# Ten blocks of the mixer input projection split at the latent and prompt boundary: 512 and 128 columns in place of 320 and 320

## The chip, the cores and the metric

The kernel runs on one core of one Trainium2 chip. The metric is device time in microseconds (us) of one execution of the whole program. A core has a matrix engine (PE here; its weight loads are listed apart, as PEld), a vector engine (DVE), a scalar engine (ACT), GpSimd (POOL) and a sync engine (SP) that issues the transfers. Each engine works through its own instructions in order, and they wait for one another by semaphores.

## The reference, cut to what matters

Two layers work on 640 tokens with 1024 features: 512 latent tokens and 128 prompt tokens, which share all weights.

```
def trunk_layer(x, cond, p, pos, ctx_kv):
    ...
    x = x + 0.5 * g1 * swiglu(h, p['wg'][0], p['wu'][0], p['wd'][0])

    h = rmsnorm(x, p['norm'][1]) * (1 + sc2) + sh2
    u = h @ p['w_in']
    ...
    u_pool, q, k, v, u_hy = jnp.split(u, [s1, s2, s3, s4], axis=-1)
    ...
    mix = jnp.concatenate([y_pool, a, y_hy], axis=-1) @ p['w_out']
    x = x + g2 * mix
    ...
    x = x + 0.5 * g3 * swiglu(h, p['wg'][1], p['wu'][1], p['wd'][1])
```

The change is in `u = h @ p['w_in']`, which has 1792 output features: 14 blocks of 128.

## The kernel before

Activations are kept with features on the 128 partitions and the 640 tokens along the free dimension, so a product's moving operand is a slice of tokens. Products are made from float32r operands (a float32 rounded to fewer bits). For accuracy every operand is split in a rounded part and its rest, and one product is three matmuls: weight-high with input-high, weight-high with input-low, weight-low with input-high. Each matmul loads its 128x128 weights anew, also where the one before used the same.

`mul` writes one half of the tokens of one block of 128 features: for each of the 8 slices `k` of the inner dimension, three matmuls that add up in one PSUM bank. A half is `HT` = 320 tokens. `gemm_steps` takes the inner dimension in two groups of four slices. For each group it loads and splits the weights (`load_weight`: a transfer, a rounding on ACT into `whi`, a subtraction on DVE into `wlo`), then calls `mul` for the first half, 12 matmuls, and for the second, 12 more; it yields after each call, so that other work can be put between.

In `mixer`, the first `MIXSKEW` = 4 of the 14 blocks are made ahead from weights that were loaded earlier (`gemm_kept`). The other ten are made in the generator `work`: two PSUM tiles, the four calls of `mul`, and two copies on ACT from PSUM into one tile `u` of 640 tokens (line 1218). Behind the blocks, `work` makes half of the output projection.

The order of the mixer's work is written out in the string `MIXP`: each letter advances one generator by a step. F is `work`, C the long convolution ("hyena": transposes `ztp`, transforms `zf` and `zfc`, products on DVE, inverse transforms `yt`), Q, K, A and X the attention (`sc`, `pt` and `o` are its tiles), P the pooling. This gives the program's order. A scheduler of the framework then orders the instructions of each engine from that, by its own estimate of their durations, so a change of shape can move instructions that the change doesn't name.

Of the kernel before, what the change touches and what calls it, by code (L numbers as in the profile page):

```python
# [19 lines left out]
LAT = 512  # L20
CTX = 128
T = LAT + CTX
HT = T // 2
# [21 lines left out]
MIXSKEW = 4  # L45
# [12 lines left out]
SEG = ((0, LAT), (LAT, T))  # L58
# [24 lines left out]
def make_consts():  # L83
# [20 lines left out]
            inv[:, i, 0, par], inv[:, i, 1, par] = np.cos(ph), np.sin(ph)  # L104
    tfi = np.concatenate([ang.reshape(P, 4, 512), inv.reshape(P, 4, 512)], axis=1).transpose(1, 0, 2).astype(np.float32)
    def parts(t):
        """Two parts of few bits each along a new axis after the partitions."""
        t = t.astype(np.float32)
        m, e = np.frexp(t)
        high = np.ldexp(np.round(m * 4096.0) / 4096.0, e).astype(np.float32)  # L110
        return np.stack([high, t - high], axis=1).reshape(P, 512)
# [19 lines left out]
    for ch in range(2):  # L131
        for half in range(2):
            w = (2, 4, 8, 16)[ch * 2 + half]
            rows = slice(64 * half, 64 * half + 64)
# [49 lines left out]
def hybrid_kernel(ctx: ExitStack, tc: tile.TileContext, a, depth=2, fc=22):  # L184
    nc = tc.nc
    V, S, G, DMA = nc.vector, nc.scalar, nc.gpsimd, nc.sync

    class PE:
        """The tensor engine; while fixed is set it issues in the order of this program."""
        last, fixed = None, False  # L190

        @classmethod
# [70 lines left out]
        return ts  # L263

    def load_tables(name, h, n, new=slot):
        """Tables of cosines and sines, each as the two parts that reduced products take."""
        ts = []
        for q in range(n):
            t = new(512, F32R, name="tab")
            DMA.dma_start(out=t.bitcast(F32), in_=a[name][h, q])  # L270
            ts.append(t.rearrange("p (h c f) -> p h c f", h=2, c=2))
        return ts

    def triple(ps, l_, r_, start, stop):
        """One product from three of parts: left and right are pairs of a rounded operand and its rest."""
        for n, (lh, rh) in enumerate(((l_[0], r_[0]), (l_[0], r_[1]), (l_[1], r_[0]))):
            PE.matmul(out=ps, lhsT=lh, rhs=rh, start=(start and n == 0), stop=(stop and n == 2))

# [43 lines left out]
            out.append((k0, k1, (hi, lo)))  # L322
        return out

    def mul(ps, wt, k0, k1, n, rhs, half, base=None):
        whi, wlo = wt
        base = k0 if base is None else base
        cs = slice(half * HT, (half + 1) * HT)
        o = ps[:, :HT]
        for k in range(k0, k1):  # L330
            wk = slice((k - base) * P, (k - base + 1) * P)
            rh, rl = rhs[k]
            PE.matmul(out=o, lhsT=whi[:, wk], rhs=rh[:, cs], start=(k == 0), stop=False)
            PE.matmul(out=o, lhsT=whi[:, wk], rhs=rl[:, cs], start=False, stop=False)
            PE.matmul(out=o, lhsT=wlo[:, wk], rhs=rh[:, cs], start=False, stop=(k == n - 1))
# [7 lines left out]
                mul(ps[half], wt, k0, k1, n, rhs, half)  # L343
        return ps

    def gemm_steps(src, rhs, ps):
        n = len(rhs)
        for k0, k1 in groups(n, 4):
            wt = load_weight(src[:, k0 * P:k1 * P], (k1 - k0) * P)
            for half in range(2):  # L350
                mul(ps[half], wt, k0, k1, n, rhs, half)
                yield 2 * (k0 > 0) + half

    def gemm_kept(kept, rhs, half):
# [3 lines left out]
            mul(ps, wt, k0, k1, n, rhs, half)  # L358
        return ps

# [1 line left out]
    condT = cp.tile([P, DC, 32], F32, name="condT")  # L362
    condb = cp.tile([P, 2, 1024], F32, name="condb")
    craw = cp.tile([P, DC, 2], F32, name="craw")
# [30 lines left out]
        done.add((l, g))  # L395

    def ada_group(l, g):
        """Modulation vectors as products of rows of the transposed weights with the condition, summed along them."""
        def load(n):
            raw = wp.tile([P, 1024], F32, tag="araw", bufs=ARAWB, name=nm("araw"))  # L400
            DMA.dma_start(out=raw, in_=a["adat"][l * 9 + g - len(AG0), n])
            ada_raw[l, g, n] = raw

        def step(n):
            raw = ada_raw[l, g, n // 2]
            i, r = n // 2, n % 2
            c, s = i // 2, i % 2
            junk = tp.tile([P, 1024], BF16, tag="junk", bufs=1, name=nm("junk"))
            with tc.issue_after(pace[0]) if pace else nullcontext():
                V.tensor_tensor_reduce(out=junk, in0=raw, in1=condb[:, r], scale=1.0, scalar=bias(l, g)[:, s, c, r:r + 1],  # L410
                                       op0=ALU.mult, op1=ALU.add, accum_out=mods[l][:, g, c, s, r:r + 1])
            if n == 2 * DC - 1:
                done.add((l, g))

        for n in range(2 * DC):
            ada_q.append(((lambda n=n: load(n // 2)) if n % 2 == 0 else None, lambda n=n: step(n)))
# [25 lines left out]
            ada_run(1)  # L442
        return mods[l][:, g].rearrange("p c s r -> p (c s) r")

# [1 line left out]
    ssq = [None, None]  # L446

    def ssq_begin():
# [9 lines left out]
    class Norm:  # L458
# [75 lines left out]
                                           in1=hi[:, c0:c1].bitcast(F32), op0=ALU.add, op1=ALU.subtract)  # L534

        def twist(self):
            """Sums of the quarters of the normed input that the seven products take; yields after each block of rows."""
            B = modv(self.key[0], self.key[2])
            ha, hb = slice(0, HT), slice(HT, T)
            t = [[(slot3(2, HT, F32R, "thi"), slot3(2, HT, F32R, "tlo")) for _ in range(2)] for _ in range(3)]  # L540
            self.t = [[(t[i][k // 2][0][:, k % 2], t[i][k // 2][1][:, k % 2]) for k in range(4)] for i in range(3)]
            self.t.append([(self.hs[k][0][:, hb], self.hs[k][1][:, hb]) for k in range(4)])
            late = []
            for k in range(4):
                for d in (k, k + 4):
                    y = self.ys[d]
                    for c0, c1, r in ((0, LAT, 0), (LAT, T, 1)):
                        S.activation(out=y[:, c0:c1], in_=y[:, c0:c1], func=AF.Identity, bias=B[:, d, r:r + 1])
                u, w = self.ys[k], self.ys[k + 4]
                s12, s34 = slot3(2, HT, name="ts"), slot3(2, HT, name="ts")  # L550
                V.tensor_tensor(out=s12[:, 0], in0=u[:, hb], in1=u[:, ha], op=ALU.subtract)
                V.tensor_tensor(out=s12[:, 1], in0=w[:, hb], in1=s12[:, 0], op=ALU.subtract)
                V.tensor_tensor(out=s34[:, 0], in0=w[:, hb], in1=u[:, hb], op=ALU.subtract)
                V.tensor_tensor(out=s34[:, 1], in0=w[:, ha], in1=s12[:, 1], op=ALU.subtract)
                for i, src in enumerate((s12[:, 0], s12[:, 1], s34[:, 0])):
                    split(src, *self.t[i][k])
                late.append(s34[:, 1])
                yield
            yield
            for k in range(4):  # L560
                split(late[k], *self.t[3][k])
            yield
# [10 lines left out]
                                       op0=ALU.mult, op1=ALU.add)  # L573
            pace[:] = [i.ins]

# [1 line left out]
    class Seven:  # L577
        """Gate and up columns of one block as seven products of sums of quarters (Winograd's form of Strassen's
        scheme): rows are gate and up, columns the two halves of the tokens, the inner dimension is cut in the middle."""

        def __init__(self, src, quart):
            self.src, self.q = src, quart
# [209 lines left out]
                            nxt.scale(0)  # L792
                            nxt.apply(0)

# [1 line left out]
    filt = {}  # L796
    INV2PI, MAGIC = 1.0 / (2.0 * math.pi), 12582912.0
    C1 = 6.28125
# [2 lines left out]
    PIC = 3.1415925  # L801

    def sine(ps, n, q, outs):
        """Both layers at once, one in each half of the partitions."""
        aa, k = slot(n, name="sa"), slot(n, name="sk")
        r = slice(0, 64 * depth)
        V.tensor_scalar(out=aa[r], in0=ps[r, :n], scalar1=fpar[r, q:q + 1], scalar2=fpar[r, q + 1:q + 2], op0=ALU.add,
# [56 lines left out]
            absd.append(ab)  # L864

    class Filter:
        """The spectra of one layer's filters of one order."""
        W = 256

        def __init__(self, l, o):  # L870
# [3 lines left out]
                filt[l] = [tp.tile([P, 4], F32, tag=t, bufs=2, name=nm("rl")) for t in ("rl512", "rl128")]  # L874

        def pair(self, win, src, c0, first=False):
            """Taps of the forward and the backward filter, their sum and difference, and their magnitudes."""
            w = slot3(1, self.W, name="win")
            S.activation(out=w[:, 0], in_=absd[self.l][:, self.oc], func=AF.Exp, scale=C("negt")[:, win:win + 1])
            ps = mix(512)  # L880
# [74 lines left out]
            DMA.dma_start(out=t.rearrange("p a b -> p (a b)"), in_=store[l, 2 * j + o])  # L955
        return flat

# [1 line left out]
    def cmul(z, k, o, prime):  # L959
        c_, s_ = (1, 0) if prime else (0, 1)  # L960
        zz = z.rearrange("p (c f) -> p c f", c=2)
# [189 lines left out]
                                   in1=t[:, c0:c1 - 1], op0=ALU.mult, op1=ALU.add)  # L1151
        return t

# [1 line left out]
    NAMES = ORDER  # L1155
    def mixer(l, cur, nxt):
        hs = cur.hs
# [52 lines left out]
        def work():  # L1210
            for m, name in enumerate(NAMES[MIXSKEW:]):
                ps = [acc(), acc()]
                for s_ in gemm_steps(a["win"][l, MIXSKEW + m], hs, ps):
                    if s_ < 3:
                        yield
                u = slot(T, name="u")
                for half in range(2):
                    S.copy(out=u[:, half * HT:(half + 1) * HT], in_=ps[half][:, :HT])  # L1218
                made[name] = u
                yield  # L1220
            while len(hhl) < 2:
# [155 lines left out]
                V.tensor_copy(out=vblk[h_][:, 3 - n:3].rearrange("p a b -> p (a b)"), in_=ps)  # L1377

        def stage_a(j):
            """Scores and softmax of the two heads that share a query tile; yields after each block of queries."""  # L1380
            qhi, qlo = qhl[j]
            m = [tiny(4, "m", 8) for _ in range(2)]
            ss = [[], []]
# [148 lines left out]
        kept, open_ = [], {}  # L1532

        def last():
            """The first output blocks' products, but for the query tile that comes last."""
            kept.extend(load_keep(a["wout"][l, d, :, 512:1024]) for d in range(4))
            yield
            for d in range(4):
                open_[d] = acc()
                mul(open_[d], kept[d][0][2], 0, 3, 4, ahl, 0)  # L1540
                yield
# [28 lines left out]
                    nxt.scale(0)  # L1570
                    nxt.apply(0)

# [1 line left out]
    DMA.dma_start(out=craw, in_=a["cond"])  # L1574
    fpar = cp.tile([P, 4], F32, name="fpar")
    DMA.dma_start(out=fpar, in_=a["fpar"])
# [228 lines left out]
```

## Time and profile before

| | |
|---|---|
| median of 3 runs | 2423.59 us (2423.26 to 2424.36) |
| profiled execution, first to last instruction (span) | 2421.6 us |
| PE busy | 2369.5 us (98% of the span), 15576 matmul records |
| PEld busy | 2243.7 us (93%) |
| DVE busy | 1922.5 us (79%) |
| ACT busy | 1096.9 us (45%) |
| share of PE in the chain that ended last | 92% |
| mean granted clock of PE | 0.990 of full |

The span is that of one execution under the profiler; the runs' times are taken without it and are 2.0 us more than the span. Matmuls are pipelined: a record's duration holds its passage through the array, while the next has already begun, so the cost of a matmul in a dense stretch is the distance from one start to the next, and a busy share of PE is no share of its peak.

### The profile page before, as it was taken

The numbers are of one execution on the slowest core, as the hardware profiler recorded it, in microseconds if no ns is written. First come the engines' busy times: TensorE is split into PE (matmuls) and PEld (weight loads), VectorE is DVE, ScalarE is ACT, GpSimd is POOL, SyncE is SP. The second block draws the span as 40 slices with busy tenths as digits, with TensorE's granted clock in tenths as the row PEclk, the third lists the DMA queues.
The fourth block names the chain that finished last, engine by engine and source line by source line (L and its number), as shares of the span: only waits on it lengthen the run. The fifth ranks groups of instructions, "written<-read, shape, count | busy, mean of one in ns | idle before, by whom it ended". The sixth has DMA issues, their size and how long they took to land.

```text
span 2421.6 us, 41063 instructions
## 1 busy us (share of the span) xinstructions
PE 2369.5 (98%) x15576; PEld 2243.7 (93%) x15576; DVE 1922.5 (79%) x3885; ACT 1096.9 (45%) x2228; POOL 18.7 (1%) x46
## 2 busy tenths in 40 slices
PE   8999999999989999999999999999998999999999
PEld 3799999999877999999999999999987789999999
DVE  7888898858887897998858778785888788567583
ACT  4653353533445553443536435253434556335251
POOL 0000000000000000000000000000000000000000
PEclk9999999999999999999999999999998999999999
DMA  9434444324411334344322433432441122222222
GB/s 330 160 110 136 135 123 156 99 81 158 135 44 43 103 120 142 127 133 150 101 72 95 127 122 108 133 113 84 135 132 63 47 88 77 81 84 78 84 68 90
DMA packets 132645, 270.36 MB, mean 112 GB/s; under 512 B 15002, under 2 KB 24924, under 8 KB 132320
## 3 DMA queue, kind: packets, MB, share of 16 engines
q1 hardware_dynamic: 132448, 267.75, 34.7%
q8 instruction: 122, 2.00, 0.3%
q14 instruction: 75, 0.61, 0.1%
HBM read 259.56 MB, written 8.13 MB: 111 GB/s over the span
## 4 chain that ended last, share of the span: by engine, by line
PE 92%; DVE 4%; issue 1%; ACT 1%; DMA 1%; POOL 0%; SPq 0%; POOLq 0%; DVEq 0%; ACTq 0%
PE mm L205 78%; PE Z L205 5%; PE o L205 1%; PE pt L209 1%; PE yt L205 1%; PE fk L205 1%; PE mx L205 1%; PE ada L205 1%; PE zf L205 1%; DVE junk L410 0%; PE rsb L205 0%; PE pm L205 0%; PE qbc L205 0%; POOL rs L482 0%; DMA ar<-in_ada 0%
## 5 line engine op out<-in xcount | busy, mean ns | idle before, releaser
L295 ACT CAST whi<-raw 128x512 fp32r<-128x512 f32 (+1 forms) x394 | 238.9, 607 | 467.8 <-PE mm L205 432.8
L205 PE MATMUL mm<-hhi,whi 128*128 128x320 f32 x1440 | 447.6, 311 | 2.9 <-ACT u L1218 2.9
L205 PE MATMUL mm<-hhi,wlo 128*128 128x320 f32 x1440 | 445.7, 310 | 0.0
L205 PE MATMUL mm<-hlo,whi 128*128 128x320 f32 x1440 | 445.3, 309 | 0.0
L205 PE MATMUL mm<-ahi,whi 128*128 128x320 f32 x1198 | 370.2, 309 | 0.0
L205 PE MATMUL mm<-alo,whi 128*128 128x320 f32 x1198 | 370.2, 309 | 0.0
L205 PE MATMUL mm<-ahi,wlo 128*128 128x320 f32 x1198 | 370.2, 309 | 0.0
L296 DVE TENSOR_TENSOR wlo<-raw,whi 128x512 fp32r<-128x512 f32 (+1 forms) x394 | 263.0, 671 | 80.8 <-ACT whi L295 78.7
L410 DVE CUSTOM_DVE_ANT_0 junk<-araw,condb,par 128x1024 bf16<-128x1024 f32 x240 | 307.1, 1280 | 5.2 <-DMA araw<-in_adat 4.1
L205 PEld LDWEIGHTS mm<-hhi,whi 128*128 128x128 f32 x1440 | 270.4, 188 | 7.7 <-ACT u L1218 4.5
L205 PEld LDWEIGHTS mm<-hhi,wlo 128*128 128x128 f32 x1440 | 270.5, 188 | 2.3 <-issue 2.3
L205 PEld LDWEIGHTS mm<-hlo,whi 128*128 128x128 f32 x1440 | 270.3, 188 | 1.0 <-issue 0.9
L205 PE MATMUL mm<-thi,whi 128*128 128x320 f32 x864 | 267.0, 309 | 0.0
L205 PE MATMUL mm<-tlo,whi 128*128 128x320 f32 x864 | 267.0, 309 | 0.0
L205 PE MATMUL mm<-thi,wlo 128*128 128x320 f32 x864 | 267.0, 309 | 0.0
L205 PEld LDWEIGHTS mm<-ahi,wlo 128*128 128x128 f32 x1198 | 224.9, 188 | 0.0
L205 PEld LDWEIGHTS mm<-alo,whi 128*128 128x128 f32 x1198 | 224.9, 188 | 0.0
L205 PEld LDWEIGHTS mm<-ahi,whi 128*128 128x128 f32 x1198 | 224.9, 188 | 0.0
L295 ACT CAST whi<-ex 128x512 fp32r<-128x512 f32 x216 | 134.3, 622 | 188.9 <-PE mm L205 177.6
L296 DVE TENSOR_TENSOR wlo<-ex,whi 128x512 fp32r<-128x512 f32 x216 | 149.0, 690 | 34.8 <-ACT whi L295 30.3
L295 ACT CAST whi<-ws 128x512 fp32r<-128x512 f32 x144 | 89.4, 621 | 163.2 <-PE mm L205 124.0
L205 PEld LDWEIGHTS mm<-thi,whi 128*128 128x128 f32 x864 | 162.2, 188 | 0.0
(263 smaller groups left out, 4710.8 us busy)
## 6 DMA issues: line engine op xcount, KB each, us to landing
araw<-in_adat SPq DMA_DIRECT2D x120, 512.0 KB, 3.8
raw<-in_wgu SPq DMA_DIRECT2D x208, 256.0 KB, 2.9
ex<-in_wgu SPq DMA_DIRECT2D x144, 256.0 KB, 2.7
raw<-in_wd SPq DMA_DIRECT2D x128, 256.0 KB, 2.7
raw<-in_win SPq DMA_DIRECT2D x56, 256.0 KB, 3.2
ar<-in_ada SPq DMA_DIRECT2D x48, 256.0 KB, 5.5
raw<-in_wd SPq DMA_DIRECT2D x64, 192.0 KB, 2.5
tab<-in_tfi SPq DMA_DIRECT2D x32, 256.0 KB, 4.1
```

The costliest lines, as they stand in the source:

```text
L205: cls.order(nc.tensor.matmul(**k))
L209: cls.order(nc.tensor.transpose(**k))
L295: S.copy(out=hi, in_=src)
L296: V.tensor_tensor(out=lo, in0=src, in1=hi.bitcast(F32), op=ALU.subtract)
L410: V.tensor_tensor_reduce(out=junk, in0=raw, in1=condb[:, r], scale=1.0, scalar=bias(l, g)[:, s, c, r:r + 1], op0=ALU.mult, op1=ALU.add, ac ...
```

## The change

`mul` and `gemm_steps` take the boundaries of the two parts as an argument `edges`, whose default is as before. `work` passes the boundaries (0, 512, 640) for its ten blocks, and copies 512 and 128 columns instead of 320 and 320. The four blocks that are made ahead, the feed-forward products and the output projection keep their halves of 320. (The diff also removes some comments.)

```
-    def mul(ps, wt, k0, k1, n, rhs, half, base=None):
+    def mul(ps, wt, k0, k1, n, rhs, half, base=None, edges=(0, HT, T)):
         whi, wlo = wt
         base = k0 if base is None else base
-        cs = slice(half * HT, (half + 1) * HT)
-        o = ps[:, :HT]
+        cs = slice(edges[half], edges[half + 1])
+        o = ps[:, :edges[half + 1] - edges[half]]
...
-    def gemm_steps(src, rhs, ps):
+    def gemm_steps(src, rhs, ps, edges=(0, HT, T)):
...
-                mul(ps[half], wt, k0, k1, n, rhs, half)
+                mul(ps[half], wt, k0, k1, n, rhs, half, edges=edges)
...
-                for s_ in gemm_steps(a["win"][l, MIXSKEW + m], hs, ps):
+                for s_ in gemm_steps(a["win"][l, MIXSKEW + m], hs, ps, (0, LAT, T)):
...
-                for half in range(2):
-                    S.copy(out=u[:, half * HT:(half + 1) * HT], in_=ps[half][:, :HT])
+                for half, (c0, c1) in enumerate(SEG):
+                    S.copy(out=u[:, c0:c1], in_=ps[half][:, :c1 - c0])
```

The two places below are on PE. A row is the source line, the operation, the output tile, the moving operand and the weights, and the shape of the output. The first is the passage from the first to the second part in the block "q3" of layer 0 (tiles `mm_6593` and `mm_6594`), before:

```order
L205 MATMUL mm_6593<-hhi_6045,whi_6597 128x320
L205 MATMUL mm_6593<-hlo_6046,whi_6597 128x320
L205 MATMUL mm_6593<-hhi_6045,wlo_6598 128x320
L205 MATMUL mm_6594<-hhi_6027,whi_6597 128x320
L205 MATMUL mm_6594<-hlo_6028,whi_6597 128x320
L205 MATMUL mm_6594<-hhi_6027,wlo_6598 128x320
```

The same place after the change:

```order
L205 MATMUL mm_6593<-hhi_6045,whi_6597 128x512
L205 MATMUL mm_6593<-hlo_6046,whi_6597 128x512
L205 MATMUL mm_6593<-hhi_6045,wlo_6598 128x512
L205 MATMUL mm_6594<-hhi_6027,whi_6597 128x128
L205 MATMUL mm_6594<-hlo_6028,whi_6597 128x128
L205 MATMUL mm_6594<-hhi_6027,wlo_6598 128x128
```

Nothing moved here; the two shapes are new, and stand in runs of twelve.

The second place is the end of the second convolution's forward transforms (`zf`, `zfc`) in layer 0, behind which the inverse transforms `yt` come; `mm_7457` and `mm_7458` are the two parts of the block "xc". Before, the last `zf` and the `zfc` stand between the block's two groups of weights, with 24 of its 48 matmuls ahead of them:

```order
L205 MATMUL mm_7458<-hhi_6045,whi_7461 128x320
L205 MATMUL mm_7458<-hlo_6046,whi_7461 128x320
L205 MATMUL mm_7458<-hhi_6045,wlo_7462 128x320
L205 MATMUL zf_7498<-zt_7149,tab_7134 128x256
L205 MATMUL zf_7498<-zt_7149,tab_7136 128x256
L205 MATMUL zfc_7539<-ztc_7162,cst 128x256 x2
L205 MATMUL mm_7457<-hhi_6051,whi_7617 128x320
```

The same transforms after the change:

```order
L205 MATMUL zf_7498<-zt_7149,tab_7134 128x256
L205 MATMUL zf_7498<-zt_7149,tab_7136 128x256
L205 MATMUL zfc_7539<-ztc_7162,cst 128x256 x2
L205 MATMUL mm_7457<-hhi_6027,whi_7461 128x512
L205 MATMUL mm_7457<-hlo_6028,whi_7461 128x512
L205 MATMUL mm_7457<-hhi_6027,wlo_7462 128x512
```

All 48 matmuls of the block now stand behind the transforms and ahead of `yt`. Layer 1 has the same move.

## Rows read from the trace of the kernel before

**Rows 1.** The profile's page: span, busy time by engine, chain that ended last.
```profile
span 2421.6 us, 41063 instructions
...
PE 2369.5 (98%) x15576; PEld 2243.7 (93%) x15576; DVE 1922.5 (79%) x3885; ACT 1096.9 (45%) x2228; POOL 18.7 (1%) x46
...
PE 92%; DVE 4%; issue 1%; ACT 1%; DMA 1%; POOL 0%; SPq 0%; POOLq 0%; DVEq 0%; ACTq 0%
```

**Rows 2.** Windows (from:to, length, busy by engine, granted clock, DMA) of the blocks' stretches.
```profile
600.00:650.00 50.00, 49.48 (x303) 42.65 (x301) 43.90 (x87) 20.29 (x39) 1.18 (x3) 1.00 0.33 105
650.00:712.00 62.00, 52.48 (x298) 44.96 (x296) 51.38 (x132) 28.43 (x70) 0.56 (x8) 0.95 0.30 99
...
1810.00:1872.00 62.00, 51.69 (x290) 44.44 (x290) 50.30 (x130) 27.93 (x69) 0.64 (x8) 0.93 0.28 95
```

**Rows 3.** Timeline of PE inside the block "q3" (start, duration in us, instruction).
```profile
592.98 0.31 PE L205 MATMUL mm<-hlo,whi 128*128 128x320 f32 x1
593.13 0.31 PE L205 MATMUL mm<-hhi,wlo 128*128 128x320 f32 x1
...
593.86 0.31 PE L205 MATMUL mm<-hlo,whi 128*128 128x320 f32 x1
```

**Rows 4.** ACT copies from PSUM by shape (count, busy us, mean ns, idle before).
```profile
L1218 ACT COPY u<-mm 128x320 f32<-128x320 f32 x40 | 15.5, 425 | 5.7 <-PE mm L205 3.7 <-DVE cw L966 2.1
...
L1094 ACT COPY zod<-zf 128x512 f32<-128x512 f32 x8 | 4.7, 586 | 18.4 <-PE zf L205 9.5 <-issue 8.9
```

**Rows 5.** Timeline of PEld, then PE, around six one-column matmuls.
```profile
811.28 0.74 PEld L205 LDWEIGHTS tot<-ones,sq 128*128 128x128 f32 x6 [1.21 <-PE mm L205]
811.95 0.19 PEld L205 LDWEIGHTS mm<-ahi,kwh 128*128 128x128 f32 x1
...
811.31 0.80 PE L205 MATMUL tot<-ones,sq 128*128 128x1 f32 x6 [0.98 <-DVE sq L455]
811.97 0.39 PE L205 MATMUL mm<-ahi,kwh 128*128 128x320 f32 x1
```

**Rows 6.** Timeline of PE: a float32r matmul behind a wait, and its successor.
```profile
550.35 0.42 PE L205 MATMUL mm<-hlo,kwh 128*128 128x320 f32 x1 [0.38 <-DVE hlo L533]
550.61 0.31 PE L205 MATMUL mm<-hhi,kwl 128*128 128x320 f32 x1
```

**Rows 7.** Timeline of PE: the attention's float32r scores, 384 and 512 columns.
```profile
706.72 0.34 PE L205 MATMUL mm<-klo,qhi 64*128 64x384 f32 x2
706.89 0.33 PE L205 MATMUL mm<-khi,qlo 64*128 64x384 f32 x2
...
696.61 0.61 PE L205 MATMUL mm<-klo,qhi 64*128 64x512 f32 x2
696.84 0.60 PE L205 MATMUL mm<-khi,qlo 64*128 64x512 f32 x2
```

**Rows 8.** Waits of PE over the whole span (waiter, releaser: us, times, longest).
```profile
PE pt L209 <- DVE sc L1351: 7.6, 4, 3.6
...
PE yt L205 <- DMA tab<-in_tfi: 5.6, 3, 2.2
...
PE mm L205 <- ACT u L1218: 2.9, 2, 1.4
...
PE yt L205 <- DVE cy L969: 2.1, 1, 2.1
```

**Rows 9.** Timeline of PE, then SP, from the last forward transforms to the inverse ones.
```profile
674.72 1.02 PE L205 MATMUL zf<-zt,tab 128*128 128x256 f32 x4
...
683.09 1.25 PE L205 MATMUL yt<-tab,pp 128*128 128x256 f32 x4 [2.24 <-DMA tab<-in_tfi]
...
680.23 2.41 SPq L261 DMA_DIRECT2D tab<-in_tfi  x4
```

**Rows 10.** Timeline of PE: a plain float32 product of 128 columns.
```profile
696.37 0.38 PE L205 MATMUL sc<-qkc 64*128 64x128 f32 x2
```

**Rows 11.** Lines by form: the same products (count, busy us, mean ns of one).
```profile
L205 PE MATMUL sc<-qkc 64*128 64x128 f32 x32 | 4.9, 284 | 0.0
```

## Prediction

> **What bounds the kernel now.** I read the page first: PE is busy 98% of the span and makes up 92% of the chain that ended last [rows 1], so a microsecond more or less of PE work counts in full unless PE was waiting there. Next the windows over the stretches in which the ten blocks are made, 600 to 712 us in layer 0 and the same some 1160 us later in layer 1. In the first 50 us there PE is busy 49.48 of 50; in the last 62 us only 52.48 (layer 1: 51.69), with DVE at 51.38 and the granted clock at 0.95 and 0.93 [rows 2]. So the reader is to see two kinds of ground: one where PE is the limit, and one where PE waits about 10 us per layer for work that DVE and the transfers finish late. Then the timeline, for what a matmul costs: records of 128x320 start at 592.98 and, six later, at 593.86, so one costs 0.1467 us although each lasts 0.31 [rows 3]. Last the waits, for what more PE work can swallow: 7.6 + 5.6 + 2.9 + 2.1 = 18.2 us, nearly all of it in the two stretches [rows 8].
>
> **The change part by part.** There are 10 blocks x 8 slices x 3 products x 2 layers = 480 pairs; the count agrees with the 40 copies of `u`, two for each of 20 blocks [rows 4]. Each pair of 320 and 320, now 2 x 0.1467 = 0.2933 us, becomes one of 512 and one of 128. The number of matmuls, weight loads and columns stays the same.
>
> *The wide one.* No row shows a float32r matmul of 512 columns over all 128 rows of the array. The nearest is the attention's scores, which use half the rows in two concurrent parts: 512 columns start 0.23 apart, 384 columns 0.17 [rows 7]. From below: 192 columns more than 320, at one a cycle of the full 2.4 GHz, is 0.1467 + 0.080 = 0.2267 us (an estimate from rows 3 and that level; in rows 7, 128 more columns cost 0.06, about one a cycle). From above: all of 0.1467 growing with the columns, 0.2347. I take 0.230.
>
> *The narrow one.* Its columns alone would cost 0.1467 - 0.080 = 0.067 us by the same slope. But every matmul brings a weight load, and what a load costs shows only where nothing covers it. Six one-column matmuls have loads that begin at 811.28, and the next load begins at 811.95: 0.112 us per load, with no column work worth the name [rows 5]. Those are plain float32 weights; the float32r weights of this kernel look the same where they are exposed: a matmul that starts right behind a wait lasts 0.42 instead of 0.31, and its successor starts 0.26 later instead of 0.147, an excess of 0.11 [rows 6]. So a load takes about 0.11 us, hides under 320 columns, and doesn't hide under 128. From below: 0.107 us (0.11 less rounding). From above: 0.125, if the 0.013 us that a 320-column matmul takes beyond its columns (0.1467 less 320 cycles of 2.4 GHz, 0.133) comes on top. I take 0.112, as the loads of rows 5 are paced with matmuls between them, the nearest thing to a run of narrow ones.
>
> A pair then costs 0.230 + 0.112 = 0.342, which is 0.0487 more; x 480 = **+23.4 us** of PE work, 11.7 per layer. Bounds: 0.2267 + 0.107 gives +19.4; 0.2347 + 0.125 gives +31.8.
>
> The weights' side speaks against a loss by one reading. Against the exposed 0.11 of [rows 6] stands a rule of the Trainium skill, "TensorE: Matmul & The Clock Gate", section "Weight-path perf modes": a fast weight load is on for 128 weights whose type isn't FP32, with a gain of up to four times for the shortest type and none for FP32; it doesn't say what float32r counts as. If that were loaded fast, the narrow matmul would cost its columns, and the sum would be 0 instead of +23.4; the exposed load in the trace doesn't look like that.
>
> *The copies.* On ACT, 2 x 425 ns become one of 128x512 and one of 128x128. A 128x512 copy from PSUM takes 586 ns; the slope between the shapes is 161 ns for 192 columns, so 128 columns take some 264, and the sum is 850 as before [rows 4]. Nothing.
>
> *What the scheduler moves.* The same instructions stand on every engine, but in places in another order. The place with a price is the second one shown above: 24 matmuls of the block "xc" stood ahead of the last `zf` and stand now between `zfc` and `yt`. In the trace, the last `zf` starts at 674.72 and `yt` at 683.09, of which PE waited 2.24 for the tables, whose transfers SP issued only at 680.23, when DVE had freed their slots [rows 9]. DVE's work from `zf` to there doesn't hang on the matmuls in between. With 12 wide and 12 narrow ones more (12 x 0.342 = 4.1 us), and 12 x 0.0487 = 0.6 us more in the 24 that stood there already, PE arrives some 4.7 us later and finds the tables. So I let the waits of `yt`, 5.6 + 2.1 = 7.7 us in both layers, be swallowed: **-7.7 us**. From below, nothing is swallowed, because DVE gets late elsewhere by the new order; from above all 18.2 us go, and with the gaps the lower clock of the last 62 us, which costs up to 0.05 x 62 + 0.07 x 62 = 7.4 us. I leave `pt`'s 7.6 and `mm`'s 2.9 as they are: they wait for chains that begin with PE's own products, and are late with PE. What is late next are the attention's scores, which PE reaches later by what is left of 11.7 us; nothing but PE's own later work waits for them.
>
> The sum: 2421.6 + 23.4 - 7.7 = 2437.3 for the profiled span; the median of the runs is 2.0 above the span, so **2439 us**.
>
> **The rivals.**
> *A, the forecast:* narrow matmuls paced by the weight load, some of the waits swallowed. For it: two independent rows for the load, PE saturated in the first part of the stretch. Against it: no row shows 128 float32r columns. 2430 to 2449.
> *B, the slack takes it:* the price is as in A, but the new order and the later PE swallow all 18.2 us of waits and some of the slow clock: 23.4 - 18.2 = +5.2, less up to 7.4: 2421 to 2429. For it: PE idles enough in [rows 2]; against it: `pt` and `mm` follow PE itself.
> *C, not slower:* the load doesn't pace the narrow matmul, because a float32r load is short or is fetched further ahead than one matmul. Place: the twelve narrow matmuls of each run; price 0.067 instead of 0.112 each; it decides as soon as the narrow one starts every 0.07 us. The pair is then 0.2934 as before and the reordering may win up to 7.7: 2416 to 2424. Rows 6 speak against it. The fast load named above would be this case, by the page.
> *D, the narrow one is run as full float32:* a plain float32 product of 128 columns is two records; two last 0.38 us together [rows 10] and one 0.284 [rows 11], so they start some 0.1 apart, and the product takes about 0.2. The pair would be 0.43, +0.137 x 480 = +66: 2490. Nothing in the profile asks for it; nothing excludes it either.
> *E, dearer and nothing swallowed:* the load and the fixed part in series, 0.230 + 0.125, +0.0617 x 480 = +29.6, with the waits as they are: 2453.
>
> **How the numbers follow.** I give A 0.62, B 0.15, C 0.10, D 0.03, E 0.10. The likeliest is A with 2439. The range from 2424 to 2453 holds A, most of B and E, and leaves out C below and D above; A's own is 2430 to 2449. This kernel's measurement tells 0.2%, 4.8 us, from no change. Slower by more than that: A, D, E and the upper edge of B, 0.78. Within: most of B and half of C, 0.15. Faster: the other half of C and the lower edge of B, 0.07.
>
> **What would show it.** Right: in runs of narrow matmuls, starts 0.11 apart and PEld without a gap; wide ones 0.23 apart; the 2.24 in front of `yt` gone; DVE and ACT busy as before; layers 0 and 1 longer by the same, between the first `u` copy and the last, and the feed-forward stretches unchanged. Wrong: narrow starts 0.07 apart (C), or 0.2 and more (D); a PE wait of some microseconds that is new, above all in front of the second convolution's products or the output projection, which now find DVE's operands late; a granted clock that falls in the narrow runs.

## The result and the profile after

| | before | after |
|---|---|---|
| first measurement, median of 3 | 2423.59 us (2423.26 to 2424.36) | 2454.01 us (2447.07 to 2454.85) |
| profiled execution, span | 2421.6 us | 2452.2 us |
| ratio to before | | 1.0109 (95%: 1.0082 to 1.0136) |

The profiled execution of after is the one of 2454.01 us. The change makes the kernel slower by some 1.1%. By the ratio that is 20 to 33 us, or 2444 to 2457 us; 2439 was predicted, with a range up to 2453, so the direction was right and the loss larger than the 15 us that were forecast.

The profile's page after, as in [rows 1]. PE's busy time grew by 38 us, that of DVE and ACT by less than one:

```profile
span 2452.2 us, 41076 instructions
...
PE 2407.6 (98%) x15576; PEld 2254.4 (92%) x15576; DVE 1923.3 (78%) x3885; ACT 1097.4 (45%) x2228; POOL 22.6 (1%) x46
...
PE 91%; DVE 5%; issue 1%; ACT 1%; DMA 1%; POOL 0%; SPq 0%; POOLq 0%; DVEq 0%; ACTq 0%
```

The forecast's first step was the price of a pair. The timeline of PE and then of PEld after, at the passage from a narrow run to a wide one in layer 0 (as in [rows 3]):

```profile
595.46 0.27 PE L205 MATMUL mm<-hhi,whi 128*128 128x128 f32 x1
...
596.01 0.28 PE L205 MATMUL mm<-hhi,wlo 128*128 128x128 f32 x1
596.13 0.45 PE L205 MATMUL mm<-hhi,whi 128*128 128x512 f32 x1
596.42 0.40 PE L205 MATMUL mm<-hlo,whi 128*128 128x512 f32 x1
596.65 0.40 PE L205 MATMUL mm<-hhi,wlo 128*128 128x512 f32 x1
...
595.39 0.19 PEld L205 LDWEIGHTS mm<-hhi,whi 128*128 128x128 f32 x1
595.51 0.19 PEld L205 LDWEIGHTS mm<-hlo,whi 128*128 128x128 f32 x1
```

From 595.46 to 596.01 are five narrow matmuls: 0.110 apart, and PEld's records are as far apart as PE's, without a gap. The wide ones are 0.23 apart. Both are the forecast's numbers. That it is the load that takes the 0.110, and not the narrow matmul itself, shows where a narrow run follows a wide one (PE, then PEld):

```profile
650.26 0.22 PE L205 MATMUL mm<-hhi,whi 128*128 128x128 f32 x1
650.32 0.28 PE L205 MATMUL mm<-hlo,whi 128*128 128x128 f32 x1
650.43 0.27 PE L205 MATMUL mm<-hhi,wlo 128*128 128x128 f32 x1
...
650.26 0.19 PEld L205 LDWEIGHTS mm<-hlo,whi 128*128 128x128 f32 x1
650.37 0.19 PEld L205 LDWEIGHTS mm<-hhi,wlo 128*128 128x128 f32 x1
```

The weights of the first narrow matmul came during the last wide one, and the second starts only 0.06 behind it. From there on each matmul starts 0.06 behind the start of its own load, and the loads are 0.11 apart.

Where the time went is read from the mixer stretches, from the sum of squares that ends one norm (tile `tot`) to the next such sum. Windows of after (length, busy by engine, granted clock, DMA), and behind them the same two of before:

```profile
561.10:829.50 268.40, 258.59 (x1479) 207.04 (x1478) 215.48 (x515) 120.87 (x292) 5.74 (x12) 0.97 0.31 102
1732.30:2001.00 268.70, 259.45 (x1479) 208.18 (x1479) 215.53 (x514) 120.24 (x292) 4.68 (x12) 0.96 0.30 97
```
```profile
555.40:811.30 255.90, 243.19 (x1479) 202.99 (x1478) 215.15 (x515) 120.52 (x292) 2.99 (x12) 0.98 0.32 107
1713.80:1970.30 256.50, 243.96 (x1479) 203.82 (x1478) 215.16 (x514) 120.34 (x292) 3.53 (x12) 0.97 0.31 102
```

Both layers are longer by 12.5 and 12.2 us, 24.7 in sum. PE's idle time (length less PE's busy time) is 9.8 and 9.3 us, against 12.7 and 12.5: 6.2 us *less*. So waiting was swallowed, and yet the stretches grew by more than the price of the pairs. The rest is the clock. Windows of after in layer 0, laid over the stretches where the granted clock was at half (1.2 instead of 2.4 GHz), and of before:

```profile
653.40:656.90 3.50, 3.50 (x16) 3.21 (x16) 3.50 (x8) 1.31 (x4) 0.00 (x0) 0.51 0.00 0
701.20:708.10 6.90, 6.28 (x15) 4.16 (x16) 6.61 (x15) 1.44 (x3) 0.28 (x4) 0.51 0.51 150
728.50:735.40 6.90, 6.58 (x14) 3.61 (x15) 6.90 (x14) 2.86 (x5) 0.00 (x0) 0.51 0.08 28
```
```profile
685.70:689.20 3.50, 3.50 (x9) 2.69 (x10) 3.31 (x6) 1.07 (x2) 0.28 (x4) 0.51 0.20 69
709.60:716.50 6.90, 4.78 (x13) 3.18 (x13) 6.89 (x17) 4.72 (x9) 0.00 (x0) 0.51 0.01 4
```

What half clock does to PE is seen inside the first of these stretches, where narrow matmuls start 0.21 apart instead of 0.110:

```profile
654.84 0.41 PE L205 MATMUL mm<-hhi,whi 128*128 128x128 f32 x1
655.05 0.41 PE L205 MATMUL mm<-hlo,whi 128*128 128x128 f32 x1
```

Over both layers the trace's records of the clock sum to 37.5 us at half in after, 23.9 in before. If half of the 13.6 more is lost, 6.8 us, then what remains of the 24.7 is 24.7 + 6.2 - 6.8 = 24.1 us: the price of the 480 pairs, of which 23.4 were forecast. This split is an estimate. Some of the time at half clock falls into waits of PE, where nothing is lost; counted only where PE was busy (35.5 us against 18.4), the clock's part is 8.5 us and the pairs' 22.3.

The waits of PE after (waiter, releaser: us, times, longest), as in [rows 8]:

```profile
PE yt L205 <- DMA tab<-in_tfi: 5.3, 2, 2.7
PE pt L209 <- DVE sc L1351: 3.6, 4, 1.6
...
PE ztp L209 <- DVE u L1295: 2.5, 2, 1.2
...
PE mm L205 <- ACT u L1218: 1.6, 2, 0.8
...
PE qbc L205 <- ACT whi L295: 1.2, 2, 0.6
PE yt L205 <- DVE cw L964: 1.1, 2, 0.6
```

The waits of `yt`, which I let go in full, fell only from 7.7 to 6.4; the one in front of the first `yt` of layer 0, 2.24 us in before, is 2.66. `pt`, which I left as it was, fell from 7.6 to 3.6.

The other 6 us of the span lie far ahead of the change. By the names of the tiles PE's order is that of before for its first 3,830 matmuls, up to 610 us. But in the profiled execution of after PE ran its matmuls at half their pace until 39.0 us; in before it did until 27.0. Timeline of before, then of after:

```profile
28.24 2.84 PE L205 MATMUL mx<-fw,h 65*128 65x512 f32 x6
```
```profile
29.88 5.49 PE L205 MATMUL mx<-fw,h 65*128 65x512 f32 x6
```

All later marks of the trace, up to the first mixer, are 5.7 to 6.1 us late for that. Whether it belongs to the change is the first experiment's question.

### The profile page after: what moved, and what is told of

Its sections match the earlier page's. It is cut to its first block, busy times and chain, and to the rows that moved or that the text cites. A ratio compares the mean times of both kernels' runs of the same rounds, so it can differ in the third digit from the quotient of the medians.

```text
span 2452.2 us, 41076 instructions
## 1 busy us (share of the span) xinstructions
PE 2407.6 (98%) x15576; PEld 2254.4 (92%) x15576; DVE 1923.3 (78%) x3885; ACT 1097.4 (45%) x2228; POOL 22.6 (1%) x46
## 4 chain that ended last, share of the span: by engine, by line
PE 91%; DVE 5%; issue 1%; ACT 1%; DMA 1%; POOL 0%; SPq 0%; POOLq 0%; DVEq 0%; ACTq 0%
PE mm L205 77%; PE Z L205 5%; PE o L205 1%; PE pt L209 1%; PE yt L205 1%; PE fk L205 1%; PE mx L205 1%; PE ada L205 1%; PE zf L205 1%; DVE junk L410 0%; ACT sc L1347 0%; PE rsb L205 0%; PE qbc L205 0%; POOL rs L482 0%; PE ztp L209 0%
## 5 line engine op out<-in xcount | busy, mean ns | idle before, releaser
L205 PE MATMUL mm<-hhi,whi 128*128 128x320 f32 (+2 forms) x1440 | 455.7, 316 | 1.6 <-ACT u L1218 1.6
L205 PE MATMUL mm<-hhi,wlo 128*128 128x320 f32 (+2 forms) x1440 | 454.5, 316 | 0.0
L205 PE MATMUL mm<-hlo,whi 128*128 128x320 f32 (+2 forms) x1440 | 453.6, 315 | 0.0
L205 PEld LDWEIGHTS mm<-hhi,whi 128*128 128x128 f32 x1440 | 271.6, 189 | 12.5 <-ACT u L1218 3.3
L296 DVE TENSOR_TENSOR wlo<-ex,whi 128x512 fp32r<-128x512 f32 x216 | 149.1, 690 | 33.7 <-ACT whi L295 29.3
## 6 DMA issues: line engine op xcount, KB each, us to landing
araw<-in_adat SPq DMA_DIRECT2D x120, 512.0 KB, 3.7
```

The costliest lines, as they stand in the source:

```text
L205: cls.order(nc.tensor.matmul(**k))
L296: V.tensor_tensor(out=lo, in0=src, in1=hi.bitcast(F32), op=ALU.subtract)
```

## The experiments

Each experiment's median and ratio are from its own measurement, with the kernel before on the same chip (2424.4 to 2425.2 us there). From one profiled execution come the sum of the two mixer stretches, PE's idle time in them (as above), the time at half clock in them, and what is left when the idle time and half of the time at half clock are taken off, which is PE's own work (an estimate, as above).

| run | columns, order | median us | ratio (95%) | mixers us | idle | half clock | rest |
|---|---|---|---|---|---|---|---|
| before | 320/320, before | 2424 to 2425 | 1 | 512.4 | 25.3 | 23.9 | 475.2 |
| after | 512/128, after | 2454.0 | 1.0082 to 1.0136 | 537.1 | 19.1 | 37.5 | 499.3 |
| e1 | 512/128, after | 2450.5 | 1.0092 to 1.0127 | 543.1 | 21.2 | 44.4 | 499.7 |
| e2 | 512/128, before | 2444.6 | 1.0062 to 1.0093 | 530.3 | 22.2 | 13.7 | 501.3 |
| e3 | 320/320, after | 2439.4 | 1.0046 to 1.0082 | 526.2 | 29.3 | 41.0 | 476.4 |
| e4 | 384/256, its own | 2431.9 | 1.0020 to 1.0045 | 519.4 | 28.6 | 34.1 | 473.8 |
| e5 | 384/256, before | 2426.2 | 1.0001 to 1.0020 | 512.0 | 23.6 | 23.9 | 476.5 |
| e6 | 448/192, before | 2432.0 | 1.0019 to 1.0045 | 522.5 | 23.2 | 27.3 | 485.7 |
| e7 | 512/128 alternating | 2457.0 | 1.0112 to 1.0151 | 543.1 | 27.2 | 37.5 | 497.1 |
| e8 | 320/320, PE before, others after | 2454.0 | 1.0104 to 1.0138 | 537.6 | 37.4 | 51.2 | 474.6 |
| e9 | 320/320, before + one move | 2427.6 | 1.0002 to 1.0024 | 514.4 | 25.6 | 27.3 | 475.1 |
| e10 | 512/128, before + one move | 2448.8 | 1.0085 to 1.0121 | 535.3 | 24.2 | 23.9 | 499.2 |
| e11 | 320/320, e9 + another move | 2428.7 | 1.0006 to 1.0025 | 517.0 | 31.9 | 20.5 | 474.9 |
| e12 | 512/128, e10 + another move | 2451.3 | 1.0095 to 1.0124 | 536.8 | 27.5 | 23.9 | 497.4 |

The last column is the table's first finding: it is 474 to 477 for all kernels with 320/320 and 384/256, in whatever order, and 497 to 501 for all with 512/128. The columns before it are less firm. After and e1 are the same program, and their profiled executions differ by 6.0 us in the mixers, 2.1 in idle time and 6.9 at half clock; differences of that size between two rows of single executions tell nothing.

**e1, the changed kernel again.**

> The changed kernel once more, unaltered. In its profile about 6 us of the 28.6 us of the span lie in the opening (27 to 39 us, long before the first changed instruction, PE at half rate there), and 24.6 us in the two mixer stretches. Theory: the opening belongs to the execution, not to the change, so that single executions of it fall into two groups some 6 us apart, near 2448 and 2454, with a median anywhere between. Rival: the opening belongs to the changed program (its code lies differently), and then all executions are near 2454.

Its five times are 2449.34, 2449.71, 2450.5, 2457.24 and 2459.7: the spread is there within one program, and not all are near 2454, as the rival has it. The 14 runs of the kernel before beside it go from 2423.08 to 2430.0. In the profiled executions of the other runs the first `tot` comes anywhere from 81.7 us (e6) to 91.9 (e4), and by the records of the clock the opening's half pace ends at 24.7 us in e2 and 28.3 in e12, both with 512 and 128 columns, and at 39.9 in e5 and 42.5 in e4, with 384 and 256. So the 6 us of the opening don't go with the change; no program was profiled with both openings, though (e1's has the late one, 38.8, as after). By the medians the change costs some 25 us.

**e2, the new shapes in the old order; e3, the new order with the old shapes.** A dependency without a semaphore was put between each instruction and the next of a written list, for PE, DVE, ACT and SP's queue in the two stretches where the orders differ:

```
+    for e, ws in json.loads(zlib.decompress(base64.b64decode(WAS))).items():
...
+            for p, q in zip(seq, seq[1:]):
+                tc.add_manual_dep(found[q], p, mybir.DependencyInfo(
+                    mybir.DependencyClass.NoSync, mybir.DependencyReason.DATA), reason="order")
```

> The changed shapes with every engine's instructions pinned to the order that the kernel before has. The step of the prediction: the new order lets 12 more pairs run ahead of yt and so swallows 7.7 us; with the old order that is lost, so this kernel takes about 7 us more than the changed one (less the opening, in both). Theory now: the order gave nothing, because DVE's chain in front of yt is late by the same; then the kernel takes the same as the changed one within 3 us, 2446 to 2450 without the slow opening, and its PE waits in front of yt are still 5 to 8 us in sum. Rival: the new order cost something of its own (some 4 us more before the waits of layer 0 and 1 than with the old), then 2440 to 2444.

> The kernel before (320 and 320 columns everywhere) with every engine's instructions pinned to the order that the changed kernel has: the order alone. The step of the prediction: 24 matmuls of xc, 3.5 us of PE work, come ahead of yt in either layer and swallow waits, up to 7.7 us in sum: 2416 to 2420. Theory now: nothing is swallowed, 2422 to 2426. Rival: the order costs some 4 us more, 2427 or so.

e2 came out at 2444.6, between the theory's 2446 to 2450 (the new order gave nothing) and the rival's 2440 to 2444 (it costs something of its own), and not above the changed kernel, as the prediction's step would have it. All theories missed e3: the order alone costs 14 us (2439.4; by the interval 11 to 20), with more idle time (+4.0) and 17 us more at half clock. The rest of its stretches is unchanged. The shapes alone cost 19 us (15 to 23). The two don't add up: together they cost some 25 (e1; 22 to 31). With the new shapes the new order costs some 6 us more than the old one (2450.5 against 2444.6, a difference just beyond the two intervals' noise), so the old one would have been the better choice for them too. The prediction had the reordering as a gain, at worst as nothing.

**e4 and e5, 384 and 256 columns.** The edit is the call's boundary and the copies':

```
-                for s_ in gemm_steps(a["win"][l, MIXSKEW + m], hs, ps, (0, LAT, T)):
+                for s_ in gemm_steps(a["win"][l, MIXSKEW + m], hs, ps, (0, 384, T)):
```

> The same blocks with 384 and 256 columns in place of 512 and 128. Theory of the load: the narrow matmul is paced by its weight load of 0.11 us only while its columns take less; 256 columns take 0.12 us (0.1467 less 64 columns at 2.4 GHz), so nothing is paced, the pair costs 0.293 as at 320 and 320, and the time is that of the kernel before, 2421 to 2427. Rival: narrow or uneven matmuls pay a fixed part of their own, or wide ones are dearer by more than their columns; then a part of the 25 us stays in proportion to the unevenness (a third of it: +8 us, 2432).

> 384 and 256 columns as in e4, with every engine's instructions pinned to the order of the kernel before. In e4 the projection's matmuls took the same time as at 320 and 320 (75.16 us in layer 0 against 75.12), and the 7 us that the two mixer stretches were longer lay in waits of PE and the half clock behind them. Theory: the shapes cost nothing and the order all of it, so this takes the time of the kernel before, 2422 to 2428. Rival: the uneven halves themselves bring the waits (the copies of u come at other moments), and it stays near e4, 2430 to 2432.

e4 came out at 2431.9, which is the rival's number and not its reason: PE's own work is that of before (473.8), and idle time and half clock make up the 7 us. The scheduler had ordered it anew; pinned to the order of before (e5), the same shapes take 1.8 us more by the medians (0.2 to 5 by the interval). The first of the rows below begins a run of twelve narrow matmuls in e5, the second one of twelve wide ones, the third the next narrow run:

```profile
597.87 0.28 PE L218 MATMUL mm<-hhi,whi 128*128 128x256 f32 x1
...
599.29 0.34 PE L218 MATMUL mm<-hhi,whi 128*128 128x384 f32 x1
...
601.38 0.28 PE L218 MATMUL mm<-hhi,whi 128*128 128x256 f32 x1
```

That is 0.118 and 0.174 for one, and 0.293 for the pair, as at 320 and 320. So uneven halves cost PE nothing by themselves as long as the narrow one's columns take longer than a weight load.

**e6, 448 and 192 columns, order of before.**

> 448 and 192 columns, order of the kernel before. Theory of the load: a floor near 0.112 us under each narrow matmul; 192 columns take 0.1467 - 0.0533 = 0.0933 us, so each pays some 0.0185 and 480 of them 8.9 us: 2432 to 2436, with narrow starts 0.11 apart as at 128 columns. Rival: a price that grows with the columns moved from one half to the other (512 and 128 with the same order: 2444.6 against 2425.2, 19.4 us for 192 columns), two thirds of it here, 13 us, and some 6 us for e5.

Measured 2432.0, 7 to 8 us more (5 to 11 by the interval, which leaves out the rival's 13), and 10 in PE's own work. The timeline of PE in a narrow run of it:

```profile
585.85 0.27 PE L218 MATMUL mm<-hhi,whi 128*128 128x192 f32 x1
585.96 0.27 PE L218 MATMUL mm<-hlo,whi 128*128 128x192 f32 x1
586.07 0.28 PE L218 MATMUL mm<-hhi,wlo 128*128 128x192 f32 x1
```

0.11 apart, as with 128 columns. A third fewer columns in the narrow half don't change its pace, and 256 columns cost PE nothing: that is a floor near 0.11, and no price in proportion to the columns moved.

**e7, wide and narrow in turn.**

```
+            for q, (w, r) in enumerate(((0, 0), (0, 1), (1, 0))):
+                for c0, c1, o in zip(edges, edges[1:], ps):
+                    PE.matmul(out=o[:, :c1 - c0], lhsT=wt[w][:, wk], rhs=rhs[k][r][:, c0:c1],
+                              start=(k == 0 and q == 0), stop=(k == n - 1 and q == 2))
```

> 512 and 128 columns, but wide and narrow matmuls alternate product by product in place of runs of twelve and twelve (the scheduler orders the engines anew). Theory: a load is fetched one matmul ahead; a narrow one gives only 0.067 us of columns to hide the load of the wide one behind it, so the pair still costs 0.34 and the time stays at 2446 to 2456. Rival: loads can run ahead by more, the wide ones' slack (0.23 - 0.11) covers the narrow ones' lack, the pair costs 0.297 and the projection 20 us less: 2425 to 2435.

2457.0, 1 us above the theory's range, and 497.1 us of PE's own work. Its timeline, where a row holds one wide and one narrow matmul:

```profile
597.01 0.50 PE L205 MATMUL mm<-hhi,wlo 128*128 128x512 f32 x2
597.35 0.50 PE L205 MATMUL mm<-hhi,whi 128*128 128x512 f32 x2
597.69 0.50 PE L205 MATMUL mm<-hlo,whi 128*128 128x512 f32 x2
```

A pair takes 0.34 in either arrangement: the 0.12 us that a wide matmul lasts beyond a load doesn't make up for what the narrow one lacks. That is the theory's number for the pair; by its reckoning a load that ran ahead by more than one matmul would have given 0.297.

**e8, PE in the old order, the others in the new.**

> 320 and 320 columns; PE's instructions in the order of the kernel before, those of DVE, ACT and the queue of SP in the order that the changed kernel has. Pinning all four took 14 us more (2439.4 against 2425.2). Theory: what costs there is that DVE and ACT come to squares, weights and copies later than PE wants them (waits of nps for qsq, yt for the tables), so the 14 us stay or grow: 2436 to 2445. Rival: the loss is PE's own (the matmuls that it put behind zfc were the cover of a later wait), and with its old order the time falls back to 2424 to 2430.

2454.0, the worst of all with 320 columns and beyond the theory's 2445: 12 us more idle time and 27 more at half clock than before. The rival is out: with its old order PE waits more for the others' new one (10.5 us for ACT's copies of `u`, 6.8 for DVE's `u` at `ztp`), and PE's own new order takes back half of that loss (e3). That the loss of e3 lies in the order of DVE, ACT and SP alone isn't shown by this, since two orders that weren't made for each other can cost something of their own. The converse, PE in the new order and the others in the old, wasn't tried.

**e9 and e10, the one move of the prediction.** All in the order of before, but in each layer:

```
-xc (24 matmuls), zf, zf, zfc x2, xc (the other 24)
+zf, zf, zfc x2, xc (24 matmuls), xc (the other 24)
```

> 320 and 320 columns; every engine in the order of the kernel before but for the one move on which the prediction's -7.7 us rests: in either layer 24 matmuls of xc stand behind zfc instead of ahead of the last zf. The step as predicted: zf comes 3.5 us earlier, PE comes to yt as late as before, DVE and the tables have 3.5 us more, and of the waits of yt (5.6 + 2.1 us) some 6 to 7.7 us go: 2416 to 2419, faster than the kernel before. Rival: the tables come when DVE has worked off a queue that doesn't begin with zf, the waits stay, and the time is 2422 to 2428. Rival: the weights of xc's second half, which wait for buffers that these 24 matmuls hold 3.5 us longer, come late, and a new wait stands at xc: 2428 to 2434.

> The same one move with 512 and 128 columns, all else in the order of the kernel before (2444.6 without the move). The step as predicted: the waits of yt (5.8 us) go, 2437 to 2440, within a microsecond or two of the time predicted for the change, 2439. Rival: the waits stay, 2442 to 2448.

Neither time is the step's. e9 is slower than before by some 3 us (2427.6 against 2424.6; 0.5 to 6 by the interval), and e10 than e2 by some 4 (2448.8 against 2444.6, with intervals that overlap). e9's time lies in the first rival's range, but the waits of `yt` didn't stay: in sum they grew from 7.7 to 9.1 us, and in e10 from 5.8 to 8.3. The one in front of the first `yt` grew from 2.24 to 3.62 us in layer 0. Its cause is in the rows of ACT, DVE and SP there, in e9:

```profile
676.93 0.62 ACT L320 CAST whi<-raw 128x512 fp32r<-128x512 f32 x1 [2.48 <-PE mm L230]
...
677.65 0.58 ACT L1119 COPY zod<-zf 128x512 f32<-128x512 f32 x1
...
677.58 0.69 DVE L321 TENSOR_TENSOR wlo<-raw,whi 128x512 fp32r<-128x512 f32 x1 [1.30 <-ACT whi L320]
...
678.87 0.68 DVE L1121 TENSOR_TENSOR zp<-zod,zf 128x512 f32<-128x512 f32 x1
...
682.05 2.41 SPq L286 DMA_DIRECT2D tab<-in_tfi  x4
```

In before, `zp` starts at 677.05 and the tables are asked for at 680.23 [rows 9]. Here (a stretch that begins 0.5 us later) PE starts the last `zf` 3 us sooner, at 671.64 against 674.72, but the moved matmuls hold a weight buffer that much longer; the cast `whi` of a later weight, the output projection's, waits 2.48 us for it, and behind that cast, in ACT's order, stands `zod`, which takes `zf` out of PSUM, and on DVE in the same way `wlo` ahead of `zp`. So what I had taken for DVE's own pace is tied to PE's matmuls. In the kernel of the change the cast waits too, but further ahead:

```profile
685.50 0.62 ACT L295 CAST whi<-raw 128x512 fp32r<-128x512 f32 x1 [3.50 <-PE mm L205]
...
686.16 0.69 DVE L296 TENSOR_TENSOR wlo<-raw,whi 128x512 fp32r<-128x512 f32 x1 [3.43 <-ACT whi L295]
...
695.24 0.68 DVE L1096 TENSOR_TENSOR zp<-zod,zf 128x512 f32<-128x512 f32 x1
...
694.49 0.57 ACT L1094 COPY zod<-zf 128x512 f32<-128x512 f32 x1
...
698.20 2.36 SPq L261 DMA_DIRECT2D tab<-in_tfi  x4
...
701.06 1.89 PE L205 MATMUL yt<-tab,pp 128*128 128x256 f32 x4 [2.66 <-DMA tab<-in_tfi]
```

DVE stands still for 3.43 us behind that cast, up to 686.16, and then works with hardly a pause through other products and the pooling to `zp` at 695.24; `zod` waits on ACT behind a copy of the pooling. The chain is of the same kind, but `zf` isn't held directly behind the cast here, and no run took the wait out of this kernel.

**e11 and e12, that cast out of the way.** On ACT the cast stands behind `zod`, on DVE its `wlo` behind `pmn`:

```
-ACT: whi, pw, zod            DVE: wlo, pw, pw, zp, ..., pmn
+ACT: pw, zod, whi            DVE: pw, pw, zp, ..., pmn, wlo
```

> e9 (320 and 320, xc moved behind zfc) with one more move: the cast whi and the rest wlo of one weight of the output projection, which in e9 waited 2.48 us for a buffer that PE's moved matmuls held, stand behind zod on ACT and behind pmn on DVE, so that zf's eviction and the products don't queue behind them. Theory: this cast is what made the tables late in e9; DVE's products start some 2.2 us sooner (1.30 of wait, 0.68 of wlo, and what zod waited), the tables are asked for near 679.9 instead of 682.05 in layer 0, the two waits in front of yt fall from 5.0 to some 2.7 us in each layer, below the 3.5 of the kernel before, and the time is 2421 to 2424. Rival: the pooling ahead of zp holds it as late, the waits stay near 5 us and the time at 2426 to 2429. The predicted step in full would be 2416 to 2419.

> The same with 512 and 128 columns, to be set beside e10 (2448.8) and e2 (2444.6). Theory: some 4 to 5 us less than e10, 2442 to 2446, with the waits in front of yt below those of e2. Rival: no change against e10, 2447 to 2450.

Neither theory came. e11's time is in its rival's range and e12's 1 us above its own, but not for the rival's reason: the waits of `yt` didn't stay, they grew to 14.0 and 11.4 us. In e11 the products start 2.24 us sooner, as the theory has it, and the tables are still later:

```profile
676.63 0.69 DVE L1121 TENSOR_TENSOR zp<-zod,zf 128x512 f32<-128x512 f32 x1 [0.16 <-ACT zod L1119]
...
683.32 1.28 DVE L321 TENSOR_TENSOR wlo<-raw,whi 128x512 fp32r<-128x512 f32 x2
...
671.94 12.42 SPq L326 DMA_DIRECT2D raw<-in_wout  x3
684.40 1.85 SPq L286 DMA_DIRECT2D tab<-in_tfi  x4
...
687.81 3.75 PE L230 MATMUL yt<-tab,pp 128*128 128x256 f32 x8 [7.02 <-DMA tab<-in_tfi]
```

The tables stand in SP's row behind three transfers of weights. These need `raw` buffers, which `wlo` frees, and `wlo` is now late: the three take until 684.36, against 678.62 in e9, and the tables go out right behind them. One wait of 7.02 us stands where e9 had 3.62 and 1.35. The time is nevertheless that of e9 within a microsecond or two: 6.2 us more idle time, 6.8 less at half clock. Half clock is counted with its half, so this leaves the mixers 2.6 us longer.

## Why the prediction was partly right

- *The price of a pair, +23.4 us.* Right, in size and cause. Starts are 0.110 and 0.23 apart, a pair takes 0.34, and PE's own work in the mixers grew by 22 to 24. That the weight load paces the narrow matmul is shown from both sides: 256 columns cost PE nothing (e5), 192 and 128 have the same 0.11 (e6), mixing wide with narrow doesn't help (e7), and a narrow matmul whose successor's load isn't behind another lets it start after 0.06 (650.26 above). Rivals C and D are excluded by it. The Trainium skill, "TensorE: Matmul & The Clock Gate", section "Weight-path perf modes", gives its fast weight load up to four times the speed for the shortest type and no gain for FP32. This trace's 0.110 for float32r weights, beside the 0.112 of plain float32 ones [rows 5], shows no such gain.
- *The copies, 0.* Right: ACT is busy 1097.4 us against 1096.9.
- *The moved matmuls swallow the waits of `yt`, -7.7 us.* This is the step that failed, and with it the sentence "DVE's work from `zf` to there doesn't hang on the matmuls in between". Made by itself the move swallows nothing: the waits of `yt` grow by 1.4 us and the time by some 3 (e9), since ACT's, DVE's and SP's rows all hold weights ahead of the transforms' work, and the weights wait for buffers that PE frees. In the changed kernel 1.3 of the 7.7 us went.
- *`pt` and `mm` stay as they are.* Wrong in the other direction: `pt` fell by 4.0 and `mm` by 1.3, and `zf`'s 2.1 is gone, while `ztp` and `qbc` got 1.4 and 1.2 more. In sum the idle time in the mixers fell by 6.2, close to the 7.7, at other places.
- *The granted clock.* My upper end let it rise as gaps close; my list of what would show the prediction wrong has it fall in the narrow runs. It fell, by 13.6 us more at half (20.5 in e1), but not for the narrow runs: their pace is 0.110 wherever the clock is full. In the profiled execution of after it fell beside the waits of `ztp`, `yt` and `pt`. In layer 0, `ztp`'s wait of 1.23 us up to 652.15 is followed by half clock from 653.4; in before that wait was half as long, and the clock stayed up. The length alone doesn't decide it: a wait of 1.43 us at `mm` (664.1) left the clock up in before. This is the term that the sum lacked: 7 to 9 us, more than the swallowed waits gave.
- *The layers alike, the feed-forward unchanged.* Right: 12.5 and 12.2, and beyond the opening nothing else moved.
- *The rivals' numbers.* The medians, 2454.0 and 2450.5 (e1), lie above A's own 2449 and near E's 2453. E's reasons didn't come: its pair was 0.355 us, and 0.34 was measured, and the waits didn't stay as they were. That the range up to 2453 reaches about as far as the result is in part luck: its upper end was E's.

So the sum that held is 24.1 - 6.2 + 6.8 = 24.7 us in the mixers, where I had 23.4 - 7.7 = 15.7. What exceeds that in the first median is the opening's 6 us, as far as one profiled execution of it tells. The new order on the whole, which I had as a gain, is a loss: 14 us with the old shapes (e3), some 6 with the new ones (e1 against e2). Why it costs so much is not shown: the place at `yt` was followed only for the one move (e9), and the other waits (for `qsq`, `u` and `m` in e3 and e8) were not.

## What to carry to other kernels

The columns of a matmul that loads its own weights are cheap only down to the length of the load: split so that both parts stay above it, and the split costs PE nothing (0.293 us a pair in e5), though the scheduler may still reorder for it (e4, 7 us). When a change of shapes lets a scheduler reorder, measure order and shapes apart, by pinning either; here each alone costs 14 to 19 us. And before letting moved work swallow a wait, follow what the waiting side is queued behind on every in-order engine, weights and their buffers included, down to the queue that issues the transfer.

## What the runs showed of the hardware that was not expected

- Gaps can cost twice. In these traces the time at half clock varies from 13.7 to 51.2 us between kernels that differ only in shapes and order, and lies beside PE's waits; but it doesn't follow their sum. e11 has 6.2 us more idle time than e9 and 6.8 less at half clock, with one long wait in place of two shorter ones; but two executions of the same program (after and e1) differ by as much at half clock. What decides it wasn't isolated.
- One and the same program has executions 8 to 10 us apart. In the two profiled ones compared above, PE runs at half pace until 27.0 or 39.0 us after its start. In before the records have the granted clock at half from 20.1 to 27.0, and full behind. In after they begin only at 39.0, with full clock; a window ahead of that reads 1.00 for want of a record, so the half pace there speaks of a half clock that isn't on record.
